# The pace of the weight sums' transfers on GpSimd, and where the last row tile is normalised

## The chip, the core and the metric

One Trainium2 chip, one core. The metric is the device time of one execution in microseconds; the time before is the median of three runs.

## What is computed

A trunk of two layers on x of 512 tokens by 2048 channels in float32. Layer 1 mixes by differential attention (8 heads) and a Mamba-2 scan, layer 2 by causal pooling over four windows; behind each stands an output projection, the residual and a layer norm. The parts that matter here:

```
def even_mixer(...):
    ...
    return jnp.concatenate([y_att, y_ssm], axis=-1) @ w_out      # 2048 x 2048
def pool_mixer(...):
    ...
    return y @ w_out                                             # 2048 x 2048
...
x = layer_norm(DEEPNORM_ALPHA * x + y, ln_g[l], ln_b[l])         # (x - mu) * rsqrt(var + eps) * g + b
```

## The kernel before

Everything that TensorE multiplies is split into a high and a low part (`split`, lines 115 to 117: a cast on ScalarE, a subtraction on VectorE), and each product is three matmuls (`mm3`, line 104). Weights come in units of 128 x 1024 (`unit`, line 119): a load on SP's queue into `raw`, and the split into `hi` and `lo`, each buffered three deep.

Both output projections are done in a form with fewer products: with the weight cut into four blocks, it needs four sums of these blocks, `t1` to `t4`. GpSimd's queue makes the sums from accumulating transfers (`presum`, line 240): 16 generators, one for each of eight parts of `wo1` and then of `wo2`, in two lanes. One generator has seven steps with 2, 2, 2, 1, 1, 1 and 1 transfers (load, accumulate, store `t1` and `t3`, accumulate, store `t2`, accumulate, store `t4`), of 512 KB each, and yields `PACE` microseconds behind each step. Its two tiles are `pre0` and `pre30` in one lane, `pre1` and `pre31` in the other, with one buffer each, in the pool `keep`.

What sets the order: a lane (`Lane`, line 57) takes generators; each `mm3` reports the matmul time that it stands for, 3 x columns / 2400 us, to all lanes (lines 109 to 113), and a lane whose wait has run down writes its generator's next step into the program at this place. `lane` and `lane2` hold the side work (the scan, attention, layer norms), `sums2` the two lanes of sums. The planner that puts the written program into each engine's list goes by the order of writing and by when it expects operands; an engine then works its list in order. `power` (line 229) raises to the power -1/2 on GpSimd. There are ten of them before the first output projection ends its first product: two in `ssm_norm` (line 506), pushed before and behind `xs_group(4)`, and one for each head (line 631). `back` (line 233) ties each transfer of a sum behind the latest power that is written (line 234), so on GpSimd's in-order queue it can't pass it.

After the eighth head's gate block the first output projection begins (line 664): `Y` with `a11`, then the sums' lanes are flushed (line 670); `V` with `a12`, then `Z` with `s1`. `s1`, `s2` and `s4` are built by `sums1` (line 677): VectorE's subtraction or addition into `sr` (line 680), then a split. `sr` (line 675) takes the places of `pre0` and `pre1`. The part of `s1` for the last two heads and the rest of the eighth head stand behind `lane.flush()` (line 685).

At the end, layer 2's output projection adds into four row tiles `xp` (128 tokens x 2048 channels). `out` is filled early with the layer norm's shift b (lines 899 to 901, for row tile 1 the first 1024 channels). Scale and shift are loaded into `g1` (four transfers) and `b1` (one) at lines 990 to 994. `finish(t)` (line 1003) normalises a row tile in four column groups of 512: ScalarE scales and shifts by the moments, VectorE multiplies by `g1`, and an accumulating store on GpSimd's queue adds to `out`. Of row tile 1, the last one, the groups in `PLAIN` (2 and 3) are added to `b1` on VectorE and stored plainly on SP's queue. Row tiles 2 and 3 are finished beside matmuls, 0 beside the last 24, 1 behind them.

Of the kernel before, what the change touches and what calls it, by code (L numbers as in the profile page):

```python
# [8 lines left out]
F32 = mybir.dt.float32  # L9
F32R = mybir.dt.float32r  # L10
AF = mybir.ActivationFunctionType
ALU = mybir.AluOpType
# [4 lines left out]
P = 128  # L17
T = 512
D = 2048
NT = T // P  # L20
# [6 lines left out]
GROUPS = (346, 346, 348, 512, 512)  # L27
WINDOWS = (2, 4, 8, 16)
NEG = -3.0e38
PLAIN = ((1, 2), (1, 3))  # L30
PACE = 9.5
AHEAD = 1000


# [49 lines left out]
def ts(j):  # L84
    return slice(j * P, (j + 1) * P)
# [3 lines left out]
def hybrid_trunk(ctx: ExitStack, tc: tile.TileContext, xT, xtok, wa, wg, wo1, wo2, prm, con, lnp, out, dbg=None):  # L89
    nc = tc.nc  # L90
    consts = ctx.enter_context(tc.tile_pool(name="consts", bufs=1))
    act = ctx.enter_context(tc.tile_pool(name="act", bufs=1))
# [111 lines left out]
    def cs(cg):  # L204
        return slice(cg * 512, (cg + 1) * 512)
# [34 lines left out]
    def presum(w, tsum, cp, ch, pool, n, after=None):  # L240
# [12 lines left out]
        back(t3, wsrc(w, 0, 1, cp, ch))  # L253
        yield PACE
        back(t, wsrc(w, 0, 1, cp, ch), True)
        back(t3, wsrc(w, 1, 1, cp, ch), True)
        yield PACE
        to(1, t)
        to(3, t3)
        yield PACE  # L260
        back(t, wsrc(w, 1, 1, cp, ch), True)
        yield PACE
        to(2, t)
# [7 lines left out]
    with ExitStack() as l1:  # L271
# [419 lines left out]
        xp = [oc.tile([P, D], F32, tag=f"xp{t}", name=f"xp{t}") for t in range(NT)]  # L691
# [102 lines left out]
    with ExitStack() as l2:  # L794
# [29 lines left out]
        with ExitStack() as mix:  # L824
            p2 = mix.enter_context(tc.tile_pool(name="pool2", bufs=2))
            yr, spill = [], []
            x1d = dram.tile([NT, P, D], F32, name="x1d")

            def residual():

                for cg in range(4):
                    ab = [p2.tile([P, T], F32, tag=f"ab{i}", name=f"ab{i}", bufs=1) for i in range(2)]
                    for i in range(2):
                        nc.gpsimd.dma_start(ab[i], lnp[0, i, cs(cg)].partition_broadcast(P))
                        nc.vector.tensor_scalar(ab[i], ab[i], ALPHA, None, op0=ALU.mult)
                    for t in range(NT):
                        xs = xp[t][:, cs(cg)]
                        nc.vector.tensor_tensor(xs, xs, ab[0], ALU.mult)
                        nc.vector.tensor_tensor(xs, xs, ab[1], ALU.add)
                        spill.append(nc.gpsimd.dma_start(x1d[t][:, cs(cg)], xs))  # L840
                        yield 5.0

            lane.push(residual())
            for g, w in enumerate(WINDOWS):
                plh = lp.tile([P, 4, T], F32R, tag="h3", name="plh")
                pll = lp.tile([P, 4, T], F32R, tag="l3", name="pll")

                def pool_block(c, vp, pad):

                    s, step = vp, 1  # L850
                    while step < w:
                        n = p2.tile([P, T + 16], F32, tag="ps", name="wsum", bufs=3)
                        lo = 2 * step - 1 if pad else step
                        nc.vector.tensor_tensor(n[:, lo:T + pad], s[:, lo:T + pad], s[:, lo - step:T + pad - step], ALU.add)
                        if not pad:
                            nc.vector.tensor_copy(n[:, :step], s[:, :step])
                        s, step = n, 2 * step
                    pl = p2.tile([P, T], F32, tag="ps", name="pl", bufs=3)
                    nc.vector.scalar_tensor_tensor(pl, in0=s[:, pad:pad + T], scalar=1.0 / w, in1=vp[:, pad:pad + T],
                                                   op0=ALU.mult, op1=ALU.subtract)  # L860
                    nc.vector.tensor_tensor(pl[:, :w - 1], s[:, pad:pad + w - 1], invt[:, :w - 1], ALU.mult)
                    nc.vector.tensor_tensor(pl[:, :w - 1], pl[:, :w - 1], vp[:, pad:pad + w - 1], ALU.subtract)
                    split(plh[:, c], pll[:, c], pl)

                if g == 0:
                    for c in range(4):
                        vblock(v0[:, c], vu[c], 256, T)
                        pool_block(c, v0[:, c], 0)
                    for c in range(4):
                        gblock(gts[:, c], gu[c], 256 if c < 2 else 0, T)  # L870
                else:
                    vu = [next_units(2) for _ in range(4)]
                    gu = [next_units(2) for _ in range(4)]
                    gts = lp.tile([P, 4, T], F32, tag="h2", name="gt")
                    for c in range(4):
                        vp = p2.tile([P, T + 16], F32, tag="vp", name="vp")
                        nc.vector.memset(vp[:, :16], 0.0)
                        vblock(vp[:, 16:], vu[c], 0, T)
                        pool_block(c, vp, 16)
                    for c in range(4):  # L880
                        gblock(gts[:, c], gu[c], 0, T)
                yr.append(lp.tile([P, 2, 2, T], F32, tag=("h0", "l0", "h1", "l1")[g], name=f"yr{g}"))
                for u in range(2):
                    hi, lo = unit(next_units(1)[0])
                    for dd in range(2):
                        d = 2 * u + dd
                        k = 4 * g + d
                        pt = bank("mm", "pgr")
                        for c in range(4):
                            o = slice((dd * 4 + c) * P, (dd * 4 + c + 1) * P)  # L890
                            mm3(pt, hi[:, o], lo[:, o], plh[:, c], pll[:, c], c == 0, c == 3)
                        y2 = p2.tile([P, T], F32, tag="ps", name="y2", bufs=3)
                        nc.vector.scalar_tensor_tensor(y2, in0=pt, scalar=pr[:, C_BGRP + k:C_BGRP + k + 1],
                                                       in1=gts[:, d], op0=ALU.add, op1=ALU.mult)
                        nc.scalar.activation(yr[g][:, u, dd], y2, AF.Copy, scale=osc[:, k:k + 1])
                if g == 0:
                    lane.flush()
                    with tc.issue_after(spill[-1].ins):
                        for t in range(NT):
                            n = 1024 if t == 1 else D  # L900
                            nc.gpsimd.dma_start(out[0, ts(t), :n], lnp[1, 1, :n].partition_broadcast(P))
                    a11 = (oc.tile([P, 8, 256], F32R, tag="xp0", name="a11h"), oc.tile([P, 8, 256], F32R, tag="xp1", name="a11l"))
                    s1 = (oc.tile([P, 8, 256], F32R, tag="xp2", name="s1h"), oc.tile([P, 8, 256], F32R, tag="xp3", name="s1l"))
                    sraw = lp.tile([P, 8, 256], F32, tag="l2", name="sraw")
                q = slice(2 * g, 2 * g + 2)
                split(a11[0][:, q], a11[1][:, q], yr[g][:, :, 0, H0])
                nc.vector.tensor_tensor(sraw[:, q], yr[g][:, :, 0, H1], yr[g][:, :, 1, H1], ALU.subtract)
                split(s1[0][:, q], s1[1][:, q], sraw[:, q])


        op = l2.enter_context(tc.tile_pool(name="op", bufs=1))
        xp = [act.tile([P, D], F32, tag=f"h{t}", name=f"xq{t}") for t in range(NT)]
# [77 lines left out]
        g1 = act.tile([P, D], F32, tag="l2", name="lng")  # L990
        for cg in range(4):
            nc.gpsimd.dma_start(g1[:, cs(cg)], lnp[1, 0, cs(cg)].partition_broadcast(P))
        b1 = act.tile([P, 1024], F32, tag="l3", name="lnb")
        nc.gpsimd.dma_start(b1, lnp[1, 1, 1024:].partition_broadcast(P))
        for cp in range(2):
            for ch in range(4):
                prod(Y[cp], a22, unit(ts2[4, cp, ch]), ch, False, True)
# [4 lines left out]

        def finish(t):
            mu, rstd = moments(op, stt[t])
            nm = op.tile([P, 1], F32, tag="nm", name="nm", bufs=4)
            nc.vector.scalar_tensor_tensor(nm, in0=mu, scalar=-1.0, in1=rstd, op0=ALU.mult, op1=ALU.mult)
            for cg in range(4):
                xs = xp[t][:, cs(cg)]
                nc.scalar.activation(xs, xs, AF.Identity, scale=rstd, bias=nm)
                nc.vector.tensor_tensor(xs, xs, g1[:, cs(cg)], ALU.mult)  # L1010
                if (t, cg) in PLAIN:
                    nc.vector.tensor_tensor(xs, xs, b1[:, cs(cg - 2)], ALU.add)
                    nc.sync.dma_start(out[0, ts(t), cs(cg)], xs)
                else:
                    nc.gpsimd.dma_start(out[0, ts(t), cs(cg)], xs, accum_op=ALU.add)
                yield 2.5

        for t in (2, 3):
            lane.push(finish(t))
# [93 lines left out]
```

## Time and profile before

| | |
|---|---|
| runs, us | 1428.81, 1424.03, 1428.55; median 1428.55 |
| profiled execution, us | 1429.07 |
| its span, us | 1427.3 |
| TensorE busy | 1394.5 us (98%), 6797 matmuls |
| VectorE, ScalarE, GpSimd busy | 841.0, 575.5, 163.3 us |
| chain that ended last | TensorE 88%, VectorE 4%, DMA 2% |
| moved by DMA | 271.26 MB, mean 190 GB/s |

The profile is that of one execution, and its times count from the start of the span. What ends an engine's idle time is inferred from semaphores: in a timeline row it stands in brackets, the idle us first, then the releaser. The granted clock is a share of TensorE's full speed. The DMA share is the mean busy share of 16 transfer engines. The program's names are those of the tiles: `pre` a sum's tile, `t` a stored sum, `raw`, `hi` and `lo` the weights, `xq` the row tiles of layer 2, `ss`, `rs` and `rstd` what a power works on.

### The profile page before, as it was taken

To read this page: it belongs to the slowest core of one execution; us is meant where nothing else is said; L and a number is where in the kernel's file an instruction comes from. 1 tells how busy PE (TensorE), PEld (TensorE's weight loads), DVE (VectorE), ACT (ScalarE), POOL (GpSimd) and SP (SyncE) were. 2 spreads that over 40 slices of the span, in tenths; PEclk is the share of its full clock that TensorE was granted. 3 is DMA by queue.
4 is the path that set the end of the run, shared out by engine and by line. 5 is a ranking of instruction groups with operands and counts; after the bars stand their busy time and mean duration, and the time that the engine had idled before them with its cause. 6 is when DMAs were issued, how large, how long until landed. Compare 5 with 4: busy or idle time off the path is not lost.

```text
span 1427.3 us, 17620 instructions
## 1 busy us (share of the span) xinstructions
PE 1394.5 (98%) x6797; PEld 1177.0 (82%) x6797; DVE 841.0 (59%) x1232; ACT 575.5 (40%) x942; POOL 163.3 (11%) x249
## 2 busy tenths in 40 slices
PE   9999999999999999999889999999999999999995
PEld 7988899888888888888668889988888888888784
DVE  6556754543455555556596797965345356567676
ACT  5232333333444444445344556433232232345443
POOL 0222220002211202121100000120000000200004
PEclk9999999999999999999989999999999999999998
DMA  7699993229946768688676555774323333556767
GB/s 269 173 313 301 283 267 107 89 77 275 298 136 203 221 160 236 192 227 237 205 245 192 191 172 168 226 259 150 104 89 104 90 102 94 187 195 204 236 206 118
DMA packets 78339, 271.26 MB, mean 190 GB/s; under 512 B 9008, under 2 KB 9136, under 8 KB 77872
## 3 DMA queue, kind: packets, MB, share of 16 engines
q1 hardware_dynamic: 48960, 166.85, 35.9%
q0 software_dynamic: 29296, 103.30, 27.4%
q8 instruction: 53, 0.87, 0.2%
q14 instruction: 30, 0.25, 0.0%
HBM read 228.17 MB, written 45.61 MB: 192 GB/s over the span
## 4 chain that ended last, share of the span: by engine, by line
PE 88%; DVE 4%; issue 2%; DMA 2%; POOL 1%; ACT 1%; DVEq 0%; POOLq 0%; ACTq 0%
PE pg L106 8%; PE pg L107 8%; PE pg L108 8%; PE pv L108 4%; PE pv L107 4%; PE pv L106 4%; PE pY L107 3%; PE pY L108 3%; PE pY L106 3%; PE pq L108 2%; PE pq L106 2%; PE pgt L108 2%; PE pk L108 2%; PE pk L107 2%; PE pxs L106 2%
## 5 line engine op out<-in xcount | busy, mean ns | idle before, releaser
L117 DVE TENSOR_TENSOR lo<-raw,hi 128x1024 fp32r<-128x1024 f32 (+3 forms) x306 | 363.7, 1189 | 379.6 <-ACT hi L116 377.8
L116 ACT CAST hi<-raw 128x1024 fp32r<-128x1024 f32 (+3 forms) x306 | 313.4, 1024 | 554.9 <-PE pg L108 91.2
L106 PE MATMUL pg<-hi,xh 128*128 128x346 f32 (+2 forms) x320 | 114.8, 359 | 0.0
L108 PE MATMUL pv<-x1h,lo 128*128 128x512 f32 (+1 forms) x320 | 111.9, 350 | 2.2 <-DVE lo L117 2.2
L106 PE MATMUL pv<-x1h,hi 128*128 128x512 f32 (+1 forms) x320 | 111.8, 349 | 0.0
L107 PE MATMUL pg<-lo,xh 128*128 128x346 f32 (+2 forms) x320 | 111.6, 349 | 0.0
L107 PE MATMUL pv<-x1l,hi 128*128 128x512 f32 (+1 forms) x320 | 111.5, 348 | 0.0
L108 PE MATMUL pg<-hi,xl 128*128 128x346 f32 (+2 forms) x320 | 111.4, 348 | 0.0
L106 PE MATMUL pg<-x1h,hi 128*128 128x512 f32 (+1 forms) x288 | 105.5, 366 | 0.0
L107 PE MATMUL pg<-x1l,hi 128*128 128x512 f32 (+1 forms) x288 | 105.4, 366 | 0.0
L108 PE MATMUL pg<-x1h,lo 128*128 128x512 f32 (+1 forms) x288 | 105.3, 366 | 0.0
L108 PEld LDWEIGHTS pv<-x1h,lo 128*128 128x128 f32 x320 | 61.2, 191 | 10.2 <-DVE lo L117 2.6
L106 PEld LDWEIGHTS pv<-x1h,hi 128*128 128x128 f32 x320 | 61.1, 191 | 7.5
L107 PEld LDWEIGHTS pv<-x1l,hi 128*128 128x128 f32 x320 | 61.1, 191 | 7.4
L107 PEld LDWEIGHTS pg<-lo,xh 128*128 128x128 f32 x320 | 60.4, 189 | 6.4 <-issue 1.4
L106 PEld LDWEIGHTS pg<-hi,xh 128*128 128x128 f32 x320 | 60.2, 188 | 6.4 <-issue 1.4
L236 POOL DMA_DIRECT2D pre<-in_wo x64 | 56.3, 947 | 76.0 <-DMA t<-pre 43.3
L108 PEld LDWEIGHTS pg<-hi,xl 128*128 128x128 f32 x320 | 60.2, 188 | 5.2
L106 PEld LDWEIGHTS pg<-x1h,hi 128*128 128x128 f32 x288 | 54.5, 189 | 8.7
L108 PEld LDWEIGHTS pg<-x1h,lo 128*128 128x128 f32 x288 | 54.4, 189 | 8.8
L107 PEld LDWEIGHTS pg<-x1l,hi 128*128 128x128 f32 x288 | 54.5, 189 | 8.6
L580 ACT ACTIVATE pm<-psc,st 128x128 f32<-128x128 f32 (+3 forms) x64 | 33.2, 524 | 69.5 <-DVE st L577 69.5
(313 smaller groups left out, 3060.7 us busy)
## 6 DMA issues: line engine op xcount, KB each, us to landing
raw<-in_wa SPq DMA_DIRECT2D x154, 512.0 KB, 3.7
pre<-in_wo POOLq DMA_DIRECT2D x96, 512.0 KB, 8.1
t<-pre POOLq DMA_DIRECT2D x64, 512.0 KB, 6.1
raw<-t SPq DMA_DIRECT2D x64, 512.0 KB, 3.4
raw<-in_wo SPq DMA_DIRECT2D x48, 512.0 KB, 3.9
raw<-in_wg SPq DMA_DIRECT2D x16, 512.0 KB, 3.6
raw<-in_wg SPq DMA_DIRECT2D x16, 346.0 KB, 5.4
xp<-in_xtok SPq DMA_DIRECT2D x16, 256.0 KB, 5.7
```

What stands on the lines that cost most here:

```text
L106: nc.tensor.matmul(o, sh, mh, start=start, stop=False, skip_group_check=more)
L107: nc.tensor.matmul(o, sh, ml, start=False, stop=False, skip_group_check=more)
L108: nc.tensor.matmul(o, sl, mh, start=False, stop=stop, skip_group_check=more)
L116: nc.scalar.copy(hi, src)
L117: nc.vector.tensor_tensor(lo, src, hi.bitcast(F32), ALU.subtract)
L236: nc.gpsimd.dma_start(dst, src, accum_op=ALU.add)
L580: nc.scalar.activation(pm[:, m, :ke], pt[:, m, :ke], AF.Exp, bias=st[:, 0, i, m:m + 1], scale=1.0, accum_out=st[:, 1, i, m:m + 1])
```

## The change

`PACE` becomes 7.0. `PLAIN` is gone: row tile 1 gets no start value in `out`, `b1` holds all 2048 channels, and `finish(1)` leaves ScalarE out: four operations subtract the mean and multiply by `g1`, four more multiply by the inverse deviation and add `b1`, each followed by a plain store on SP's queue. The other row tiles keep the old form.

```diff
-PLAIN = ((1, 2), (1, 3))
-PACE = 9.5
+PACE = 7.0
...
-                        for t in range(NT):
-                            n = 1024 if t == 1 else D
-                            nc.gpsimd.dma_start(out[0, ts(t), :n], lnp[1, 1, :n].partition_broadcast(P))
+                        for t in (0, 2, 3):
+                            nc.gpsimd.dma_start(out[0, ts(t)], lnp[1, 1].partition_broadcast(P))
...
-        b1 = act.tile([P, 1024], F32, tag="l3", name="lnb")
-        nc.gpsimd.dma_start(b1, lnp[1, 1, 1024:].partition_broadcast(P))
+        b1 = act.tile([P, D], F32, tag="l3", name="lnb")
+        nc.gpsimd.dma_start(b1, lnp[1, 1].partition_broadcast(P))
...
         def finish(t):
             mu, rstd = moments(op, stt[t])
-            nm = op.tile([P, 1], F32, tag="nm", name="nm", bufs=4)
-            nc.vector.scalar_tensor_tensor(nm, in0=mu, scalar=-1.0, in1=rstd, op0=ALU.mult, op1=ALU.mult)
+            if t != 1:
+                nm = op.tile([P, 1], F32, tag="nm", name="nm", bufs=4)
+                nc.vector.scalar_tensor_tensor(nm, in0=mu, scalar=-1.0, in1=rstd, op0=ALU.mult, op1=ALU.mult)
+                for cg in range(4):
+                    xs = xp[t][:, cs(cg)]
+                    nc.scalar.activation(xs, xs, AF.Identity, scale=rstd, bias=nm)
+                    nc.vector.tensor_tensor(xs, xs, g1[:, cs(cg)], ALU.mult)
+                    nc.gpsimd.dma_start(out[0, ts(t), cs(cg)], xs, accum_op=ALU.add)
+                    yield 2.5
+                return
+
             for cg in range(4):
                 xs = xp[t][:, cs(cg)]
-                nc.scalar.activation(xs, xs, AF.Identity, scale=rstd, bias=nm)
-                nc.vector.tensor_tensor(xs, xs, g1[:, cs(cg)], ALU.mult)
-                if (t, cg) in PLAIN:
-                    nc.vector.tensor_tensor(xs, xs, b1[:, cs(cg - 2)], ALU.add)
-                    nc.sync.dma_start(out[0, ts(t), cs(cg)], xs)
-                else:
-                    nc.gpsimd.dma_start(out[0, ts(t), cs(cg)], xs, accum_op=ALU.add)
-                yield 2.5
+                nc.vector.scalar_tensor_tensor(xs, in0=xs, scalar=mu, in1=g1[:, cs(cg)], op0=ALU.subtract, op1=ALU.mult)
+            for cg in range(4):
+                xs = xp[t][:, cs(cg)]
+                nc.vector.scalar_tensor_tensor(xs, in0=xs, scalar=rstd, in1=b1[:, cs(cg)], op0=ALU.mult, op1=ALU.add)
+                nc.sync.dma_start(out[0, ts(t), cs(cg)], xs)
+            yield 0.0
```

## Rows read from the trace of the kernel before

**Rows 1.** The page: busy us, share of the span and instructions, by engine.

```profile
PE 1394.5 (98%) x6797; PEld 1177.0 (82%) x6797; DVE 841.0 (59%) x1232; ACT 575.5 (40%) x942; POOL 163.3 (11%) x249
```

**Rows 2.** Waits of TensorE: waiter <- releaser; us in total, times, longest.

```profile
PE pZ L107 <- DVE lo L117: 6.0, 1, 6.0
```

**Rows 3.** Timeline, TensorE, first output projection: start, us, what [idle before <-releaser].

```profile
711.58 0.80 PE L107 MATMUL pZ<-lo,a12h 128*128 128x512 f32 x1 [5.98 <-DVE lo L117]
...
735.27 0.80 PE L106 MATMUL pZ<-hi,s1h 128*128 128x512 f32 x1 [4.85 <-ACT s1h L116]
```

**Rows 4.** Stretches: us, busy of each engine (instructions); clock, DMA share, GB/s.

```profile
711.60:716.80 5.20, 5.20 (x12) 4.11 (x13) 5.20 (x8) 2.26 (x4) 0.00 (x0) 0.50 0.74 235
716.80:730.00 13.20, 13.20 (x59) 10.89 (x58) 13.20 (x19) 7.27 (x9) 0.00 (x0) 1.00 0.98 344
735.30:740.80 5.50, 5.50 (x12) 3.94 (x13) 5.50 (x10) 1.22 (x2) 0.00 (x0) 0.50 0.26 101
```

**Rows 5.** Timeline, VectorE, the same place.

```profile
699.61 0.68 DVE L772 TENSOR_TENSOR sr<-yTs 128x512 f32<-128x512 f32 x1
...
709.10 0.69 DVE L680 TENSOR_TENSOR sr<-yTs,yTa 128x512 f32<-128x512 f32 x1 [8.81 <-DMA t<-pre]
...
733.88 0.69 DVE L680 TENSOR_TENSOR sr<-yTs,yTa 128x512 f32<-128x512 f32 x1
```

**Rows 6.** Timeline, GpSimd, sums and powers.

```profile
211.93 0.53 POOL L238 DMA_DIRECT2D pre<-in_wo  x1 [1.95 <-DMA t<-pre]
...
319.72 1.04 POOL L231 TENSOR_TENSOR rs<-rs,nhalf 128x4 f32<-128x4 f32 x1 [107.26 <-DVE rs L505]
...
362.47 1.04 POOL L231 TENSOR_TENSOR rs<-rs,nhalf 128x4 f32<-128x4 f32 x1 [5.99 <-DVE rs L505]
...
535.23 1.03 POOL L231 TENSOR_TENSOR ss<-ss,nhalf 128x4 f32<-128x4 f32 x1 [23.36 <-DVE ss L630]
...
693.24 1.03 POOL L231 TENSOR_TENSOR ss<-ss,nhalf 128x4 f32<-128x4 f32 x1 [21.79 <-DVE ss L630]
...
704.13 0.55 POOL L238 DMA_DIRECT2D t<-pre  x1 [3.07 <-DMA pre<-in_wo]
```

**Rows 7.** Stretches of the sums, and of VectorE's backlog.

```profile
52.00:212.00 160.00, 160.00 (x848) 140.37 (x847) 100.68 (x141) 58.33 (x103) 42.85 (x68) 1.00 1.00 288
212.00:272.00 60.00, 60.00 (x354) 55.54 (x354) 30.51 (x36) 22.60 (x45) 0.47 (x1) 1.00 0.35 108
710.00:740.00 30.00, 23.57 (x81) 18.33 (x82) 30.00 (x43) 14.41 (x19) 0.00 (x0) 0.78 0.79 271
```

**Rows 8.** DMA issues: out<-in, queue, count, KB, median us to landing.

```profile
x1d<-xp POOLq DMA_DIRECT2D x16, 256.0 KB, 4.3
...
lnb<-in_lnp POOLq DMA_DIRECT2D x1, 512.0 KB, 10.0
...
out<-xq SPq DMA_DIRECT2D x2, 256.0 KB, 5.9
```

**Rows 9.** A stretch beside the loading of `lnb`.

```profile
1345.00:1350.00 5.00, 4.98 (x22) 3.67 (x20) 2.17 (x3) 1.05 (x1) 0.00 (x0) 1.00 0.86 338
```

**Rows 10.** Timeline, TensorE, behind that load.

```profile
1354.80 0.53 PE L107 MATMUL pY<-lo,cxp 128*128 128x512 f32 x1 [1.86 <-DVE lo L117]
...
1358.54 0.40 PE L107 MATMUL pY<-lo,cxp 128*128 128x512 f32 x1
```

**Rows 11.** Groups, shapes apart, 52 to 212: busy us, mean ns | idle before.

```profile
L299 DVE SCALAR_TENSOR_TENSOR xo<-cth,acc 128x512 f32<-128x512 f32 x8 | 5.5, 691 | 3.6 <-ACT cth L298 3.6
```

**Rows 12.** Timeline, VectorE, the last layer norm.

```profile
1395.83 4.94 DVE L1010 TENSOR_TENSOR xq<-xq,lng 128x512 f32<-128x512 f32 x8
...
1414.47 0.15 DVE L211 TENSOR_SCALAR rstd<-mv 128x1 f32<-128x1 f32 x1
...
1419.97 0.69 DVE L1012 TENSOR_TENSOR xq<-xq,lnb 128x512 f32<-128x512 f32 x1
```

**Rows 13.** Timeline, SP's queue, the last stores.

```profile
1419.36 1.67 SPq L1013 DMA_DIRECT2D out<-xq  x2
```

## The prediction

> **What bounds the kernel now.** I read the page first: TensorE is busy for 1394.5 us, 98% of the span [rows 1]. So a change pays only where TensorE stands still or runs slowly, or at the end, after its last matmul. The second view is the list of TensorE's waits; its longest is 6.0 us in one piece, for a weight split on VectorE [rows 2]. The third, TensorE's timeline, puts that halt at 711.58, in the first output projection, and a second one of 4.85 us, for the high part of `s1` on ScalarE, at 735.27 [rows 3]. The reader should then look at the granted clock by stretch. From 716.8 to 730.0 it is 1.00, and 59 matmuls start in 13.20 us, 0.224 each; in the 5.20 us behind the first halt and the 5.50 behind the second it is 0.50, the lower of its two levels (1.2 instead of 2.4 GHz), and only 12 start in each [rows 4]. So the halts cost more than the wait list says: 5.98 + (5.20 - 12 x 0.224 = 2.51) and 4.85 + (5.50 - 2.69 = 2.81), together 16.2 us.
>
> Where they come from is on VectorE's timeline: it sits 8.81 us, until 709.10, on the subtraction of line 680, whose releaser is a store `t<-pre` [rows 5]. The subtraction writes `sr`, which takes over the buffers of the weight sums, so it can start only when the last sum is stored. VectorE works its list in order: the weight splits queued behind line 680 wait too, ScalarE waits for the subtraction, and TensorE runs out of split weights. The instruction just ahead, line 772 at 699.61, belongs to the much later `s3`; that it stands there says that the planner expected the wait and filled it [rows 5]. Last comes GpSimd's timeline: the last power runs at 693.24, and the last store of a sum is issued at 704.13 [rows 6]. A sum's transfers are tied behind the latest power (line 234), so the last four wait for the last head's power, although they have nothing to do with it.
>
> **Part 1, the pace.** `PACE` 9.5 -> 7.0 changes no transfer, only how many are written into the program between two powers. I counted by adding up what `mm3` gives the lanes: 3 x columns / 2400 us for each call. Up to the first power (line 506 in `ssm_norm(0)`) this gives 206.7 us; a sum has 7 steps with 10 transfers. At 9.5 that is 22 steps in a lane, 64 transfers in both; then 14, 14, 8, 12, 6, 10, 8, 12 and 8 between the ten powers, and four after the last. GpSimd's timeline has just these counts (among them the 64 that end with 211.93 and the four after 693.24) [rows 6], so I trust the same count for 7.0: 30 steps, 88 transfers ahead of the first power, then 16, 16, 16, 12, 10, and the last two behind the sixth power, at 535.23 [rows 6]. The last store moves from 704 to about 545 us, some 150 us before `sr` is wanted.
>
> What is removed is the whole 16.2 us if nothing else is late there. Late next is VectorE itself: it has work without a gap in 710 to 740, 30.00 of 30.00 us [rows 7]. It gets to this work 8.81 us earlier, and the subtractions for the heads that are done (0.69 each, and their splits) can move further ahead. TensorE reaches `s1` earlier too, by 8.5. I leave 1.0 us for a split that then comes late; the bounds are 0 and the whole second halt, 7.7 us (a rival, below).
>
> The 24 transfers that move ahead of the first power run behind the 64. These took the stretch of 52 to 212, with four copies the 68 instructions of GpSimd in it [rows 7], 2.5 us each; so the 88 end near 272, 48 us before the power at 319.72 [rows 6]. The stretch that they move into, 212 to 272, had the transfer engines at a share of 0.35; in the one before, with the same mixture at 1.00 and 288 GB/s, TensorE was busy for 160.00 of 160.00 us [rows 7]. I cost this at nothing; the cover is the weights' buffering, three deep, and without it each late weight would be a halt like the above. Between the later powers stand up to 16 transfers instead of 14. The tightest place is the second power, for which GpSimd had waited 5.99 us [rows 6]: two more transfers at 2.5 us still fit. Nothing, then; the upper bound is a rival.
>
> **Part 2, the shift vector whole.** `b1` grows from 512 to 1024 KB, the fifth of five transfers that GpSimd issues there. It collides with weights: the 512 KB took 10.0 us to land [rows 8], 338 GB/s were moved from 1345 to 1350 [rows 9], and TensorE halted 1.86 us until 1354.80 and then ran 9 steps to 1358.54 in 3.74 instead of 2.02 us, 3.6 us in all [rows 10]. The other half is at most 0.52 MB / 338 GB/s = 1.55 us of halt and three more slow steps (0.6). It lands late, when the next weights may already be there, so the lower bound is 0. I take +1.0, between the ends, as the tail of `b1` meets the weight behind the halt. The prefill of `out` shrinks by 512 KB where nobody waits for it.
>
> **Part 3, the last tile.** Taken away for tile 1: `nm`, four ScalarE activations, four multiplications, two additions, two accumulating stores. Added: eight `scalar_tensor_tensor` on VectorE and two more plain stores from SP. The first four need the mean alone, so they run beside the power. Price: the same form with both tensors in SBUF is line 299, 691 ns for 128x512 [rows 11]; eight independent operations of line 1010 took 4.94 us, 0.617 each [rows 12]. From the end of line 211 at 1414.62 the eight end at 1414.62 + 4.94 = 1419.6, or at 1420.15 if none overlaps. VectorE ended at 1420.66 [rows 12]. So 0.5 to 1.05 us are gained up to the last store. Before, SP's two left from 1419.36 on [rows 13] and landed after a median of 5.9 us [rows 8], beside two accumulating ones. Now four plain ones leave 0.62 us apart. A plain store of this size took 4.3 us in a quieter stretch [rows 8]. Bounds of the part: -3.0 (1.05, and 5.9 - 4.3 = 1.6, rounded up) and +0.7 (0.5 gained; 1.05 MB at 338 GB/s take 3.1 us where they are issued over 1.9, 1.2 lost). I take -1.5, nearer to VectorE's own gain.
>
> Here a rule speaks against the change. The Trainium skill (Vector Engine (DVE) Microarchitecture Reference, Points that are easy to get wrong) says that this instruction with two SBUF sources that are not bf16 runs at half throughput. By that each of the eight would take twice its time and the part would be a loss of some 3 us. The trace does not agree: line 299 has such sources and takes 691 ns [rows 11].
>
> **The sum.** 1427.3 - 16.2 + 1.0 + 1.0 - 1.5 = 1411.6 for the span. The profiled execution took 1429.07, 1.77 outside the span: 1413.4. It stands 0.52 over the median of 1428.55, so 1412.9, forecast as 1413.
>
> **The rivals.**
> - *The second halt stays.* VectorE's list is so dense that `s1`'s third quarter, at 733.88 before [rows 5], is late again. For it: no gap in 710 to 740. Against: that step stood late because of the wait that goes. Only 8.5 of 16.2 us come back: 1428.55 - 8.5 + 1.0 - 1.5 = 1419.5.
> - *No gain.* The transfers are not placed as counted, or the loads of the token rows beside the weights hold up the same splits. Against: the counts of before agree, and the weights bore full transfer engines [rows 7]. Then only parts 2 and 3 count: 1428.55 + 1.0 - 1.5 = 1428.
> - *Slower: powers behind transfers.* If the 16 transfers take longer than the time between two powers, each power comes late and the head's transposes stop TensorE. It decides where the two extra ones take over 5.99 us and the 5.5 us that the program leaves between power and transposes, 11.5 us instead of 5. Four powers late by 6 us beyond that: 1428.55 - 16.2 + 24 + 1.0 - 1.5 = 1436.
> - *Two passes.* Each of the eight operations with two SBUF tensors takes 0.617 us twice, 4.9 us more: 1413 + 4.9 = 1418. Line 299 speaks against it.
>
> **How the numbers follow.** Both halts gone: 0.72. Second halt stays: 0.14. No gain: 0.07. Slower: 0.04. Two passes: 0.03. The likeliest gives 1413, its own range 1409 (no allowance, nothing for `b1`, -3.0 at the end) to 1416 (+2.15 and +0.7). To leave out no more than 2 in 10 it must reach the first rival: 1409 to 1420. A measurement of this kernel can tell about 0.5%, 7 us, from no change, so faster means below 1421.4: 0.72 + 0.03 + nearly all of 0.14 = 0.88; same 0.08; slower 0.04.
>
> **What would show it.** On GpSimd's timeline 88 transfers before the first power and none after the last; line 680 on VectorE with no wait for a store, and before 700; neither halt among TensorE's waits, and its granted clock at the higher level from 690 to 800. Near 1340 a halt of 2 to 3.5 us. At the end eight operations in 5 us, the first four before the power is back. Wrong would be: a wait of TensorE for `s1` that is still there (first rival), a power whose releaser is a transfer (third), or 1.2 us for one of the eight (fourth).

## The result and the profile after

| | before | after |
|---|---|---|
| median, us | 1428.20 | 1409.62 |
| lowest to highest of four | 1424.03 to 1428.81 | 1406.62 to 1411.53 |
| profiled execution, its span | 1429.07, 1427.3 | 1406.62, 1404.9 |

The ratio is 0.9874, with a 95% interval of 0.9848 to 0.9900: 18.0 us less by the ratio (14.3 to 21.7); the two medians lie 18.6 apart. Forecast were 1413 and 15.6 us less.

The reader can place the gain with GpSimd's timeline alone, because its powers and loads stand at fixed points of the program: the first power, the last head's power, the first power of layer norm 1, the load of `g1`, and the first and the last power of layer norm 2. For the kernel before, the first two are in [rows 6]; the rest of them, before:

```profile
806.84 0.86 POOL L231 TENSOR_TENSOR rstd<-rstd,nhalf 128x1 f32<-128x1 f32 x1 [102.16 <-DVE rstd L211]
...
1338.34 2.12 POOL L992 DMA_DIRECT2D lng<-in_lnp  x4 [91.61 <-PE pZ L108]
...
1393.49 1.08 POOL L231 TENSOR_TENSOR rstd<-rstd,nhalf 128x1 f32<-128x1 f32 x2 [52.50 <-DVE rstd L211]
...
1414.70 0.73 POOL L231 TENSOR_TENSOR rstd<-rstd,nhalf 128x1 f32<-128x1 f32 x1
```

and all of them after, with the fourth power (at 455.46) beside them, where GpSimd now has least time to spare:

```profile
318.90 1.04 POOL L230 TENSOR_TENSOR rs<-rs,nhalf 128x4 f32<-128x4 f32 x1 [44.15 <-DVE rs L504]
...
455.46 1.03 POOL L230 TENSOR_TENSOR ss<-ss,nhalf 128x4 f32<-128x4 f32 x1 [0.52 <-DVE ss L629]
...
692.11 1.01 POOL L230 TENSOR_TENSOR ss<-ss,nhalf 128x4 f32<-128x4 f32 x1 [38.49 <-DVE ss L629]
789.54 0.84 POOL L230 TENSOR_TENSOR rstd<-rstd,nhalf 128x1 f32<-128x1 f32 x1 [96.42 <-DVE rstd L210]
...
1320.40 2.12 POOL L990 DMA_DIRECT2D lng<-in_lnp  x4 [91.11 <-DVE lo L116]
...
1373.88 1.08 POOL L230 TENSOR_TENSOR rstd<-rstd,nhalf 128x1 f32<-128x1 f32 x2 [50.84 <-DVE rstd L210]
...
1395.10 1.00 POOL L230 TENSOR_TENSOR rstd<-rstd,nhalf 128x1 f32<-128x1 f32 x1
```

The lead over before is 0.8 us at the first power, 1.1 at the last head's, 17.3 at layer norm 1, 17.9 at the load of `g1`, 19.6 at layer norm 2's first and last power, and 22.4 at the end of the span. So 16.2 us come between the last head's power and layer norm 1 (113.60 us before, 97.43 after), 1.7 beside the loads of `g1` and `b1` (a matter of the clock, below), 2.8 behind the last power, and the rest (1.7) in places that the change doesn't touch. The profiled executions lie 22 us apart and the medians 18.6: the one of after was the fastest of its four.

What answers to [rows 2] and [rows 3], TensorE's waits after:

```profile
PE pv L107 <- DVE lo L116: 2.9, 2, 2.5
...
PE pY L106 <- DVE lo L116: 1.4, 1, 1.4
...
PE pY L105 <- ACT hi L115: 0.6, 1, 0.6
```

Neither halt of the first output projection is in the list. The stretch 700 to 740 (us, then busy TensorE, weight load, VectorE, ScalarE, GpSimd; clock, DMA share, GB/s) shows TensorE without a gap at the full clock, and VectorE at 36.81 of 40 us instead of 30.00 of 30.00 [rows 4, 7]:

```profile
700.00:740.00 40.00, 40.00 (x178) 33.15 (x177) 36.81 (x48) 20.07 (x24) 0.00 (x0) 1.00 0.87 297
```

VectorE's subtraction of line 680 (now 679) still waits for a store, but elsewhere: the first one runs at 539.12, 170 us earlier than before, right behind the last stores of the sums (issued from 535.40), and waits 2.96 us for them instead of 8.81. TensorE is busy without a gap there (15.00 of 15.00 us from 530 to 545). The part for the last heads follows at 698.77 without a wait [rows 5]:

```profile
539.12 0.69 DVE L679 TENSOR_TENSOR sr<-yTs,yTa 128x512 f32<-128x512 f32 x1 [2.96 <-DMA t<-pre]
...
698.77 0.68 DVE L679 TENSOR_TENSOR sr<-yTs,yTa 128x512 f32<-128x512 f32 x1
```

At the end, VectorE's timeline, then SP's and the DMA issues (KB each, median us to landing), for [rows 8, 12, 13]:

```profile
1394.86 0.15 DVE L210 TENSOR_SCALAR rstd<-mv 128x1 f32<-128x1 f32 x1
1394.93 2.73 DVE L1016 SCALAR_TENSOR_TENSOR xq<-xq,mv,lng 128x512 f32<-128x512 f32 x4
1397.58 2.73 DVE L1019 SCALAR_TENSOR_TENSOR xq<-xq,rstd,lnb 128x512 f32<-128x512 f32 x4
```

```profile
1398.36 2.32 SPq L1020 DMA_DIRECT2D out<-xq  x4
```

```profile
lnb<-in_lnp POOLq DMA_DIRECT2D x1, 1024.0 KB, 10.8
out<-xq SPq DMA_DIRECT2D x4, 256.0 KB, 3.5
```

The first four operations start at 1394.93, ahead of the power at 1395.10; they outlast it, and the other four start at 1397.58, when it has long been back. The eight end 5.30 us after the end of line 211's counterpart (1395.01), 0.74 us sooner than before (1420.66 - 1414.62 = 6.04). The stores land in 3.5 us instead of 5.9.

### The profile page after: what moved, and what is told of

Its sections match the earlier page's. It is cut to its first block, busy times and chain, and to the rows that moved or that the text cites. A ratio compares the mean times of both kernels' runs of the same rounds, so it can differ in the third digit from the quotient of the medians.

```text
span 1404.9 us, 17616 instructions
## 1 busy us (share of the span) xinstructions
PE 1385.0 (99%) x6797; PEld 1170.6 (83%) x6797; DVE 841.3 (60%) x1233; ACT 572.3 (41%) x938; POOL 161.6 (12%) x246
## 3 DMA queue, kind: packets, MB, share of 16 engines
q1 hardware_dynamic: 49248, 167.37, 36.5%
```

## The experiments

The theory: the last four transfers of the sums, tied behind the last power, hold the buffers of `sr`, and both halts come from that; the rest of the gain is at the end. Each run's ratio is to the kernel before on the same chip (medians 1426.6 to 1427.5), and the us less are worked out from it.

**The pace alone.**

```diff
-PACE = 9.5
+PACE = 7.0
```

> The kernel before with PACE 7.0 and nothing else. Theory (the last four transfers behind the last power hold the buffers of `sr`, and both halts of TensorE near 711 and 735 come from that): both halts gone, 16.2 us less in that place, the end of the kernel as before; 1428.2 - 16.2 = 1412, ratio 0.9887. Rival 1 (the second halt is VectorE's own backlog): 8.5 us less, 1420. Rival 2 (most of the measured 18 us lies in the last tile): under 10 us less, 1419 or more.

Measured: 1410.72, ratio 0.9881 (0.9866 to 0.9896), 17.0 us less. Between the last head's power and layer norm 1 lie 97.45 us, as in the changed kernel:

```profile
691.95 1.01 POOL L231 TENSOR_TENSOR ss<-ss,nhalf 128x4 f32<-128x4 f32 x1 [38.50 <-DVE ss L630]
789.40 0.83 POOL L231 TENSOR_TENSOR rstd<-rstd,nhalf 128x1 f32<-128x1 f32 x1 [96.45 <-DVE rstd L211]
```

**The rest of the change alone.** The changed kernel with

```diff
-PACE = 7.0
+PACE = 9.5
```

> The changed kernel with PACE back at 9.5: whole shift vector and the last tile on VectorE alone. Theory: both halts near 711 and 735 as before; at the end VectorE is done 0.7 us earlier and the last store lands 2 us sooner after its issue, 2.8 us less; the whole shift vector costs 0 to 1; 1428.2 - 2.3 = 1426, ratio 0.9984. Rival 2: 8 us or more of the gain is here, 1420. Rival 4 (the larger load of the shift vector costs what the tail gains): 1428.

Measured: 1425.76, ratio 0.9991 (0.9981 to 1.0001), 1.3 us less. Both halts are back, and the same stretch takes 113.61 us:

```profile
693.08 1.03 POOL L230 TENSOR_TENSOR ss<-ss,nhalf 128x4 f32<-128x4 f32 x1 [22.03 <-DVE ss L629]
...
806.69 0.85 POOL L230 TENSOR_TENSOR rstd<-rstd,nhalf 128x1 f32<-128x1 f32 x1 [101.00 <-DVE rstd L210]
```

The two parts add up: 17.0 + 1.3 against 18.0. Nearly everything is the pace, and rivals 1 and 2 fall. Rival 4 does not fall by the times, whose interval reaches 1.0001; the profiles put the gain at the end at 3.1 us and the cost of the larger load at 1.0 to 1.5 (both below).

**The buffer or the crowd.** The kernel before, with all transfers where they were, but `sr` on the places of the third sum's tiles, which are stored earlier:

```diff
-        sr = [keep.tile([P, 2, 2, 256], F32, tag=f"pre{n}", name="sr")[:, i] for n in range(2) for i in range(2)]
+        sr = [keep.tile([P, 2, 2, 256], F32, tag=f"pre3{n}", name="sr")[:, i] for n in range(2) for i in range(2)]
```

> The kernel before, PACE 9.5 and all transfers where they were, but `sr` takes the places of the tiles for the third sum, whose last store is issued a step or more ahead of the last power. Theory: what costs is the buffer, not the transfers, so both halts go although four transfers still run behind the last power; 16 us less, 1412. Rival 3 (what costs is the crowding of the transfer engines between 690 and 710, four sums' transfers beside weights and token rows): halts stay or shrink by a third at most, 1423 or more.

Measured: 1414.47, ratio 0.9907 (0.9893 to 0.9921), 13.3 us less. The four transfers still run behind the last power, and line 680 no longer waits for them (GpSimd's timeline, VectorE's, then TensorE's):

```profile
692.22 1.03 POOL L231 TENSOR_TENSOR ss<-ss,nhalf 128x4 f32<-128x4 f32 x1 [22.35 <-DVE ss L630]
...
703.89 0.55 POOL L238 DMA_DIRECT2D t<-pre  x1 [4.14 <-DMA pre<-in_wo]
792.47 0.86 POOL L231 TENSOR_TENSOR rstd<-rstd,nhalf 128x1 f32<-128x1 f32 x1 [88.03 <-DVE rstd L211]
```

```profile
658.92 0.68 DVE L680 TENSOR_TENSOR sr<-yTs,yTa 128x512 f32<-128x512 f32 x1
```

```profile
711.37 0.50 PE L107 MATMUL pZ<-lo,a12h 128*128 128x512 f32 x1 [0.76 <-DVE lo L117]
...
715.21 0.50 PE L107 MATMUL pZ<-lo,a12h 128*128 128x512 f32 x1 [0.77 <-DVE lo L117]
```

The stretch takes 100.25 us: 13.35 of the 16.2 us were the buffer. The other 2.8 come with the four transfers that still stand there, beside the weights and the token rows: three small halts (0.24, 0.76 and 0.77 us), and slower steps between them at a granted clock of 1.00. The five weight loads issued from 690 to 722 landed after a median of 8.5 us, against 4.9 in the changed kernel, and ScalarE's split waited for them (DMA issues, then ScalarE's timeline):

```profile
raw<-in_wo SPq DMA_DIRECT2D x5, 512.0 KB, 8.5
```

```profile
709.01 1.05 ACT L116 CAST hi<-raw 128x1024 fp32r<-128x1024 f32 x1 [3.57 <-DMA raw<-in_wo]
```

So the crowding that rival 3 speaks of has a share. The theory named the main cause and left out this second one.

**The smallest step.** The kernel before with

```diff
-PACE = 9.5
+PACE = 9.0
```

> The kernel before with PACE 9.0. By the count of lanes 68 transfers stand ahead of the first power instead of 64, six behind the ninth power and none behind the tenth. Theory: it is a step, not a slope: with none behind the last power the whole 16 us come, 1412. Rival 5 (what counts is how many transfers move ahead of the first power): 4 of the 24 moved, a sixth of the gain, 1425.

Measured: 1416.29, ratio 0.9920 (0.9907 to 0.9934), 11.4 us less: neither of the two. From the last power to layer norm 1 it takes 97.42 us, the full gain, but the last power comes at 699.41, 7.3 us late (GpSimd's timeline; VectorE's; TensorE's waits):

```profile
699.41 1.03 POOL L231 TENSOR_TENSOR ss<-ss,nhalf 128x4 f32<-128x4 f32 x1 [30.80 <-DVE ss L630]
796.83 0.84 POOL L231 TENSOR_TENSOR rstd<-rstd,nhalf 128x1 f32<-128x1 f32 x1 [96.40 <-DVE rstd L211]
```

```profile
669.32 0.69 DVE L680 TENSOR_TENSOR sr<-yTs,yTa 128x512 f32<-128x512 f32 x1 [5.80 <-DMA t<-pre]
```

```profile
PE pat L593 <- DVE pm L585: 3.2, 1, 3.2
PE psc L574 <- ACT pm L580: 1.9, 1, 1.9
```

With the last six transfers behind the ninth power, line 680 is planned for the middle of the eighth head, waits 5.80 us for the store there, and the head's softmax stands behind it on VectorE. So it is neither a slope in the number that moves ahead (4 of 24 brought 11.4 of 17 us) nor enough that nothing stands behind the last power: the buffers must be free where the planner puts the first subtraction.

**The other side.** The changed kernel with `PACE` 6.0, 5.0 and 4.0.

> The changed kernel with PACE 6.0: 100 transfers ahead of the first power, then 20, 20, 16 and 4. At 2.4 us each (152 took from 53 to 417 with PACE 4.0) the 100 end near 293, ahead of 319; the 20 behind it end some 5 us behind the second power, whose transposes stand 9 us of matmul time later. Theory (a step, and no slope, between 88 and about 110): no halt after 300, same as the changed kernel, 1409. Other: a halt of 5 us or more at the transposes of the second power, 1414.

> The changed kernel with PACE 5.0: 120 transfers ahead of the first power. At 2.4 us each they end near 341, 22 us behind the 319 at which the first power is wanted; with PACE 4.0 a power 98 us late stopped TensorE for 97.4 us. Theory: one halt of 15 to 22 us at the transposes behind the first power, and half clock behind it, 1425 to 1435. Other (the planner's order leaves more room): halt under 10 us, 1420 or less.

> The changed kernel with PACE 4.0: by the count 152 transfers stand ahead of the first power. At 2.5 us each they end at 52 + 380 = 432, 113 us behind the time at which the first power is wanted (319). Third rival of the prediction (powers behind transfers stop TensorE at the transposes): halts of 50 to 100 us after 320, 1460 or more. Other rival: the planner, which knows that the power is late, moves the transposes back, and nothing is wanted from them before the output projection at 660: within 3 us of the changed kernel, 1410 to 1413.

Measured: 1424.19 (0.9974, 0.9962 to 0.9985), 1457.32 (1.0208, 1.0189 to 1.0226) and 1508.01 (1.0565, 1.0542 to 1.0588). The gain of some 18 us shrinks to 4 with the next microsecond of pace, and then it is a loss. The theories for 6.0 and 5.0 were missed, and both came out slower than theory or rival said; for 4.0 the prediction's third rival came. For 6.0, GpSimd's timeline, VectorE's (two rows) and TensorE's waits:

```profile
319.74 1.04 POOL L230 TENSOR_TENSOR rs<-rs,nhalf 128x4 f32<-128x4 f32 x1 [8.63 <-DVE rs L504]
...
373.06 1.06 POOL L230 TENSOR_TENSOR rs<-rs,nhalf 128x4 f32<-128x4 f32 x1
```

```profile
362.20 0.30 DVE L504 TENSOR_SCALAR rs<-ssq 128x4 f32<-128x4 f32 x1 [0.85 <-ACT junk L501]
...
478.94 0.69 DVE L679 TENSOR_TENSOR sr<-yTs,yTa 128x512 f32<-128x512 f32 x1 [5.74 <-DMA t<-pre]
```

```profile
PE pyt L514 <- DVE y L508: 7.0, 1, 7.0
PE psc L573 <- ACT pm L579: 3.8, 1, 3.8
```

The operand of the second power is there at 362.50, the power runs at 373.06, and TensorE stops 7.0 us at the transposes behind it. The second halt, 3.8 us, is that of PACE 9.0 over again: the first subtraction is planned into a head's softmax and waits 5.74 us there for the last store. For 5.0 and 4.0, TensorE's wait and the first power:

```profile
PE pyt L514 <- DVE y L508: 46.1, 2, 36.5
```

```profile
356.65 1.08 POOL L230 TENSOR_TENSOR rs<-rs,nhalf 128x4 f32<-128x4 f32 x1
```

```profile
PE pyt L514 <- DVE y L508: 97.4, 1, 97.4
```

```profile
416.94 1.08 POOL L230 TENSOR_TENSOR rs<-rs,nhalf 128x4 f32<-128x4 f32 x1
```

A first power that is 37 or 98 us late (its operand was there at 319.8 and 319.1) stops TensorE for 36.5 or 97.4 us: there is next to no cover in front of these transposes. The planner doesn't move them back. The price of 2.4 us for each transfer was too low for 6.0 and 5.0: from 53 us on, the 100 took 2.58 each and the 120 took 2.53.

**Plain stores, old form.** The changed kernel with the last tile normalised as before, and four plain stores:

```diff
+            nm = op.tile([P, 1], F32, tag="nm", name="nm", bufs=4)
+            nc.vector.scalar_tensor_tensor(nm, in0=mu, scalar=-1.0, in1=rstd, op0=ALU.mult, op1=ALU.mult)
             for cg in range(4):
                 xs = xp[t][:, cs(cg)]
-                nc.vector.scalar_tensor_tensor(xs, in0=xs, scalar=mu, in1=g1[:, cs(cg)], op0=ALU.subtract, op1=ALU.mult)
-            for cg in range(4):
-                xs = xp[t][:, cs(cg)]
-                nc.vector.scalar_tensor_tensor(xs, in0=xs, scalar=rstd, in1=b1[:, cs(cg)], op0=ALU.mult, op1=ALU.add)
+                nc.scalar.activation(xs, xs, AF.Identity, scale=rstd, bias=nm)
+                nc.vector.tensor_tensor(xs, xs, g1[:, cs(cg)], ALU.mult)
+                nc.vector.tensor_tensor(xs, xs, b1[:, cs(cg)], ALU.add)
                 nc.sync.dma_start(out[0, ts(t), cs(cg)], xs)
```

> The changed kernel, but the last tile in its old form (ScalarE, then a multiplication and an addition on VectorE) with four plain stores. Theory (of the 2.8 us won at the end 0.7 come from VectorE's form and 2 from stores that are plain and land in 3.5 instead of 5.9 us): landing stays at 3.5, VectorE's end comes 1.2 us later after the last matmul than in the changed kernel; 1411, ratio 0.988. Rival 6 (the short landing comes from the spacing of 0.62 us that VectorE's form gives the stores): landing at 5 or more, 1413.

Measured: 1411.15, ratio 0.9882 (0.9864 to 0.9900). The last power, the stores on SP's queue, and their landing:

```profile
1399.96 0.56 POOL L230 TENSOR_TENSOR rstd<-rstd,nhalf 128x1 f32<-128x1 f32 x1
```

```profile
1403.05 4.07 SPq L1021 DMA_DIRECT2D out<-xq  x4
```

```profile
out<-xq SPq DMA_DIRECT2D x4, 256.0 KB, 2.5
```

From the last power to the end of the span it takes 10.14 us. With two accumulating stores it was 12.60, 12.90, 12.47 and 12.69 (before and the three runs with its end), mean 12.67; with VectorE alone 9.80, 9.63, 9.57, 9.52, 9.73, 9.19, 9.58 and 9.45 (after and the seven runs with its end), mean 9.56. So of 3.1 us, 2.5 come from storing plainly and 0.6 from VectorE's form, as far as the one profile of the form between them tells. Rival 6 falls: 1.2 us apart the plain stores land even sooner, in 2.5 us.

**The changed kernel once more.**

> The changed kernel once more, beside the two others: 1409.6, ratio 0.987, halts of TensorE of 0.6 and 1.4 us near 1335.

Measured: 1408.13, ratio 0.9868 (0.9851 to 0.9886). In its profile there is one halt beside the loads of `g1` and `b1`, and the clock falls behind it (TensorE's timeline, then the stretch), where the first profile of the same kernel had two halts (0.57 and 1.43 us) and kept the full clock:

```profile
1337.64 0.80 PE L106 MATMUL pY<-lo,cxp 128*128 128x512 f32 x1 [1.77 <-DVE lo L116]
```

```profile
1330.00:1340.00 10.00, 8.12 (x30) 6.00 (x29) 5.98 (x8) 4.20 (x4) 0.00 (x0) 0.88 0.73 268
```

**The loads spread, in two ways.** First by steps of matmul time, in a lane:

```diff
-        for cg in range(4):
-            nc.gpsimd.dma_start(g1[:, cs(cg)], lnp[1, 0, cs(cg)].partition_broadcast(P))
...
-        nc.gpsimd.dma_start(b1, lnp[1, 1].partition_broadcast(P))
+        def scale_shift():
+            for i, w in enumerate((g1, b1)):
+                for cg in range(4):
+                    nc.gpsimd.dma_start(w[:, cs(cg)], lnp[1, i, cs(cg)].partition_broadcast(P))
+                    yield 2.5
+        lane.push(scale_shift())
```

> The changed kernel, but the scale and shift vectors are loaded as eight transfers of 256 KB, one every 2.5 us of matmul time, instead of five at once. Theory (these loads, 2 MB at once, make the weights late): the two halts of TensorE near 1335, 2.0 us, go; 2 us less than the changed kernel, 1407.6, ratio 0.986. Rival 7 (the weight held back for the last product makes the halts, not these loads): halts stay, same as the changed kernel. Rival 8 (spread loads meet more weights, each a little): several halts below 1 us up to the last layer norm, same or 1 us more.

Measured: 1407.76, ratio 0.9862 (0.9848 to 0.9877), the same as the changed kernel. The forecast time was met, but not for its reason, and the run tells nothing on the theory, since the loads didn't spread: GpSimd's queue stood at the first of them until the place of `g1` came free, and then issued all eight in a row:

```profile
1320.79 2.12 POOL L994 DMA_DIRECT2D lng<-in_lnp  x4 [91.03 <-PE pZ L107]
1322.90 2.12 POOL L994 DMA_DIRECT2D lnb<-in_lnp  x4
```

So a second time with a true operand in front:

```diff
+        nc.gpsimd.tensor_copy(b1[:, :1], stt[3][:, 1, :1])
         nc.gpsimd.dma_start(b1, lnp[1, 1].partition_broadcast(P))
```

> The changed kernel, but GpSimd writes one column of `b1` from the statistics of row tile 3 (second column group) before it loads `b1`, so this load of 1 MB starts some 20 us later, near 1341, when the scale vector has landed. From the first load of the scale vector to the first power of the last layer norm, four profiles with half of `b1` took 52.7 to 55.2 us, mean 53.5, and four with the whole 53.5 to 56.4, mean 55.2. Theory (2 MB at once make the weights late): the halts near 1335 shrink to less than 1.3 us in all and none comes near 1345; this stretch takes 53 or less, 1.5 to 2 us less than the changed kernel, ratio 0.9855. Rival 8 (the load meets as many weights later): a new halt of 1 us or more near 1345 to 1350, same as the changed kernel.

Measured: 1408.11, ratio 0.9872 (0.9852 to 0.9893). `b1` waits (GpSimd's timeline), and the halts near 1335 are gone; two new ones, 0.93 us in all instead of 2.0, stand behind the load of `b1` (TensorE's):

```profile
1340.97 1.04 POOL L992 COPY lnb<-bst 128x1 f32<-128x1 f32 x1 [16.96 <-DVE bst L946]
```

```profile
1349.92 0.50 PE L105 MATMUL pY<-hi,cxp 128*128 128x512 f32 x1 [0.17 <-ACT hi L115]
1351.18 0.50 PE L106 MATMUL pY<-lo,cxp 128*128 128x512 f32 x1 [0.76 <-DVE lo L116]
```

From the load of `g1` to layer norm 2 it takes 52.56 us, less than any of the seven with the whole of `b1` at once (53.48 at the least, at the same clock of 1.00). The median shows nothing of it: 1408.11 against 1408.13. One profile agrees with the theory, and in the new halts, though below 1 us, with rival 8 too; that the kernel became faster is not shown.

## Why the prediction was right, point by point

- **Both halts, 16.2 us.** The place gave 16.17 (113.60 - 97.43), and the pace alone 17.0. That the transfers wait behind the last power and hold `sr` was the main cause: 13.35 us with nothing else changed. The prediction counted the whole on this one wait; 2.8 us of it come with the four transfers' own place beside the weights, a cost that it had not named (its rival spoke of the token rows' loads). One of its signs did not hold: line 680 still waits for a store, 2.96 us at 539, where nobody needs the result yet.
- **The allowance of 1.0, and the rival of the second halt (0.14).** Not needed. VectorE is nearly as full as before from 700 to 740, but the first subtraction is done 170 us earlier (539.12 against 709.10), as the planner was expected to do.
- **The transfers between the powers, at nothing.** Right at 7.0 ahead of the first power: GpSimd waited 44.15 us for it (forecast 48). But the second power was not the tightest place, as the prediction had it. There 16 transfers left 4.6 to 6.5 us of idle time in six profiles, 14 left 5.9 to 6.2 in three, so the two more cost less than 1 us and not 5. Ahead of the fourth power 16 transfers stand where 8 stood, in 39.4 us; GpSimd's idle time there fell from 14.15 us to 0.52, 0.5 to 1.8 in six profiles. By the prediction's own 2.5 us for each transfer this power would have come late. That it did not was luck, and the changed kernel stands 0.5 us from a late power; what a late one costs at this place no run shows. The slower rival's cover of 5.5 us was too large as well: PACE 6.0 shows 7.0 us of halt for 10.6 us of lateness at the second power, 3.6 of cover, and at the first power there is 0.4. The 2.5 us hold as a mean (52.3 us for the 20 behind the first power at 6.0), but not as the price of one more: GpSimd's issues wait for one another's data.
- **`b1` whole, +1.0.** From the load of `g1` to layer norm 2's first power, four profiles with the half took 55.15, 53.47, 52.86 and 52.71 us, seven with the whole in one load 53.48, 55.97, 56.35, 54.88, 54.40, 55.77 and 54.29: means 53.5 and 55.0, +1.5. They overlap, and the clock is mixed in: over this stretch it was 0.97 in one of the four and in four of the seven, and 1.00 in the others. At 1.00 the means are 53.0 and 54.1, +1.0; at 0.97 they are 55.2 and 55.7. The two profiles compared first, before and after, say the opposite (-1.7), because the clock fell in the one and not in the other. Sign and size were right as far as eleven profiles tell.
- **The end, -1.5.** The term that was mis-sized: 3.1 by twelve profiles, where the lower bound was 3.0. VectorE's part was as computed (0.74 of 0.5 to 1.05; the eight operations take 0.66 us apiece, between 0.617 and 0.69), but the landing was taken to stay near 5.9, and it fell to 3.5. The row of 4.3 us for a plain store had said so; I chose by VectorE's gain instead.
- **Half throughput.** The Trainium skill's sentence (Vector Engine (DVE) Microarchitecture Reference, Points that are easy to get wrong) says that this instruction with two SBUF sources that are not bf16 runs at half throughput, and does not say of what. The prediction took it for twice the time of a plain multiplication, and that did not come: four operations with two float32 sources in SBUF took 2.73 us, 0.68 each, against 0.617 for plain multiplications in a row, which have two such sources too [rows 12]; with one of its sources in PSUM (line 709 before) it takes 0.68 as well. Beside an operation with a single float32 source in SBUF (line 509 before, four of 128x512 in 1.68 us, 0.42 each) it takes 1.6 times as long; whether the sentence means that, no run here shows.

With the measured terms the sum is -16.2 + 1.5 - 3.1 = -17.8, against -18.0 measured.

## What to carry to other kernels

When a buffer is taken over, look at what its last writer queues behind: a transfer tied to an unrelated instruction on an in-order queue makes the next owner wait for that instruction. Moving such transfers ahead pays when the buffers are free where the planner puts the next owner's first operation, and it turns into a loss as soon as they no longer fit in front of an instruction that others wait for; so measure the idle time in front of each such instruction, not the mean price of a transfer. Price a store at the end by the landing of the same kind of store, and compare single profiles only over places where their clocks agree.

## What was not expected of the hardware

- Two executions of one kernel differ in the granted clock behind a halt of about the same size: 1.00 behind 0.57 and 1.43 us in the one, 0.88 in the stretch of a halt of 1.77 us in the other. What decides this is open. From the load of `g1` to layer norm 2 the first took 53.48 us, the second 54.88.
- A plain store of 256 KB lands (medians) in 5.7 to 6.1 us beside accumulating stores issued 2 us earlier, in 3.0 to 3.5 beside its like at 0.6 us, and in 2.5 at 1.2 us.
